# Token sums of a fast down projection made beside gate-up, the gated result added in DRAM, and wider modulation sums

## The chip, the cores and the metric

The program runs on one core of one Trainium2 chip. The metric is the device time of one execution in microseconds, as a median of several executions. TensorE is called PE here, VectorE DVE, ScalarE ACT, GpSimd POOL, and SyncE SP; SP does nothing but issue transfers.

## The reference

One layer of a diffusion backbone works on 640 tokens (512 latent tokens and 128 context tokens) of width 2048, all in float32. What matters here is the conditioning vector and the second half of the layer:

```
mod   = silu(c) @ w_ada + b_ada               # 6 parts of 2048, once for latent, once for context
x     = x + gate1 * mixed                     # mixed: attention and convolution through w_out
h2    = rms_norm(x, g_norm2) * (1 + scale2) + shift2
gte, up = split(h2 @ w_gate_up)               # 2 x 5632 columns
x     = x + gate2 * ((silu(gte) * up) @ w_down)
y     = rms_norm(x, g_final)
```

## The kernel before, in words

Features lie on the partitions and tokens on the free axis: a tile of 128 features holds two halves of 320 tokens (256 latent and 64 context tokens each). Every float32 operand of a product is split into a rounded high part (a float32r copy, made by ACT, line 143) and the remainder (a subtraction by DVE, line 144), and three matmuls (high-high, high-low, low-high) make the product.

Gate-up and down are computed with a 2x2 block scheme with seven products in place of eight (`seven`, line 715). It needs sums of the weights, made in `weights` (lines 702 to 712) by DVE, and sums of two token tiles: from the tiles b1 and b2 the four halves t3, n1, t2 and t4 (in `splits`, line 650). A *unit* is one weight tile of 512 KB and 42 matmuls that use 14 token tiles, the high and low parts of seven tiles for each of two pairs. The pool R has 57 slots of a token tile's size, and four units fill 56 of them.

The stages follow one another: an early part, the convolution projections, attention, the out projection in two halves of 16 rounds, gate-up (44 rounds of four units), down (26 *visits* of one to four units, 80 units in all), and a tail of 16 rounds in two passes, which multiplies the last four of the 44 middle tiles with a piece of w_down that is left over, adds it, and makes the final norm.

Around the change the work goes as follows:

- **Modulation** (`ada2`, line 256): the columns of w_ada for gate1, shift2, scale2 and gate2 are summed on DVE, 512 columns at a time. In each of 16 row blocks a multiply-add for each of two conditioning vectors goes over a tile of 128x512. `background(n)`, called by each weight split, hands out steps of this work at a rate that belongs to the stage (`RATES`). Twelve of the sixteen column blocks are handed out in the convolution and the first half of the out projection, four in gate-up.
- **Gate-up** stores each gated tile in DRAM (`mid`, line 749, on ACT's queue).
- **Down** joins a new unit every second visit. Four tiles of `mid` are loaded on SP's queue (line 767), POOL makes the four sums of each pair (lines 655 to 658), ACT and DVE split them (lines 143 and 144). A visit's seven products become two tiles by one ACT copy and seven DVE operations (lines 777 to 784), and both are stored or added in DRAM to `y` by a transfer on POOL's queue (lines 787 and 789).
- **Between down and tail** `y` and the residual `x1` come back from DRAM, DVE multiplies by gate2 and adds (line 802), four `mid` tiles are loaded and split, and 16 weight tiles for the tail are loaded and split (lines 804 to 815).

The order on each engine and queue is not the source order. A planner simulates the program and issues what is ready and lies first in the source; `after(x)` forces an instruction to stand behind x on its engine. Tiles of a tag share a number of buffers, and a tile waits until the buffer's earlier user is done.

Of the kernel before, what the change touches and what calls it, by code (L numbers as in the profile page):

```python
# [16 lines left out]
P = 128  # L17
# [12 lines left out]
WINDOW = KT // 2  # L30
S = 512
# [45 lines left out]
def _emit(nc, tc, pool, dram, a):  # L77
# [13 lines left out]

    def brief(n, name):

        return bpool.tile([P, n], F32, name=name, tag="D", bufs=bufs["D"])
# [25 lines left out]
    def two(ap, n):  # L120
        return ap.rearrange("p (j n) -> p j n", j=2)
# [54 lines left out]
    cc = pool.tile([P, KT, 2], F32, name="cc")  # L176
# [78 lines left out]

    def ada2(b):
        acc = [brief(512, "acc") for _ in range(2)]
        for q in range(8):
            ws = [T1(F32, (P, 512), "aw") if bufs is SECOND else brief(512, "aw") for _ in range(2)]
            for kk in range(2):  # L260
                nc.sync.dma_start(ws[kk], a["ada2"][b, q, :, kk])
            for kk in range(2):
                k = 2 * q + kk
                with after(newest[V]):
                    for v in range(2):
                        if k == 0:
                            V.tensor_scalar(acc[v], ws[kk], sc[:, k, v:v + 1], None, op0=ALU.mult)
                        else:
                            V.scalar_tensor_tensor(acc[v], ws[kk], sc[:, k, v:v + 1], acc[v],  # L269
                                                   op0=ALU.mult, op1=ALU.add)  # L270
                yield
        yield
        yield
        with after(newest[T]):
            pb = psB()
            for v in range(2):
                for j in range(4):
                    T.matmul(pb[32 * j:32 * j + 32, v * P:(v + 1) * P], ones[:, 0:32], acc[v][:, j * P:(j + 1) * P],
                             start=True, stop=True)
            ev = T2(F32, (P, 256), "ev")  # L280
            A.copy(ev, pb[:, 0:256])
        yield
        with after(newest[T]):
            for v in range(2):
                T.transpose(pb[:, 256 + v * P:256 + (v + 1) * P], ev[:, v * P:(v + 1) * P], ident)
            col = pb[:, 256:512].rearrange("p (v j x) -> p j v x", v=2, j=4)[:, :, :, 0]
            fs = slice(4 * b, 4 * b + 4)
            V.tensor_tensor(mod2[:, fs, :], col, bada[:, 4 * b:4 * b + 4, :], op=ALU.add)
            if 8 <= b < 12:
                g = cst("g2", KT, 2)[:, 4 * (b - 8):4 * (b - 8) + 4, :]  # L290
                V.scalar_tensor_tensor(mod2[:, fs, :], mod2[:, fs, :], 1.0, g, op0=ALU.add, op1=ALU.mult)

    def ada2_steps(blocks, overlap=True):
        prev = iter(())
        for b in blocks:
            gen = ada2(b)
            if not overlap:
                yield from gen
                continue
            for _ in range(16):  # L300
                next(gen)
                next(prev, None)
                yield b
            prev = gen
        for _ in prev:
            yield b

    steps = ada2_steps((0, 1, 2, 3, 4, 8, 5, 9, 6, 10, 7, 11))
# [341 lines left out]
    def splits(xs, n, wide):  # L650


        (b1, b2), e = xs, G if wide else V
        ta, tb = T1(F32, (P, 2, n)), T2(F32, (P, 2, n))
        e.tensor_tensor(ta[:, 0], b1[:, 1], b2[:, 1], op=ALU.subtract)
        e.tensor_tensor(ta[:, 1], b1[:, 1], b1[:, 0], op=ALU.subtract)
        e.tensor_tensor(tb[:, 0], b2[:, 1], ta[:, 1], op=ALU.subtract)  # L657
        e.tensor_tensor(tb[:, 1], b2[:, 0], tb[:, 0], op=ALU.subtract)  # L658
        out = {}
        one = R(F32R, (P, 2, n))  # L660
        split(one[:, 0], one[:, 1], b1[:, 0])
        out["b11"] = one[:, 0], one[:, 1]
        for t, names in ((b2, ("b21", "b22")), (ta, ("t3", "n1")), (tb, ("t2", "t4"))):
            hi, lo = R(F32R, (P, 2, n)), R(F32R, (P, 2, n))
            split(hi, lo, t)
            for k, name in enumerate(names):
                out[name] = hi[:, k], lo[:, k]
        return out

# [4 lines left out]
    for m in range(KT):  # L674
        add_gated(proj(a["w_out"][m], na, (1,)), ra, m)
        add_sq(ssq, x1[m], m == 0, G if m < KT - 2 else V)

        u = (T1 if m % 2 else T2)(F32, (P, 2, 322))
        for v, f in PARTS:
            A.mul(f(u), f(x1[m]), mod2[:, 32 + m, v:v + 1])  # L680
        G.tensor_copy(u[:, 0, 320:322], mod2[:, 16 + m, :])
        G.memset(u[:, 1, 320:322], 0.0)
        nc.scalar.dma_start(two(x1d[m], 320), x1[m])
        us.append(u)
        if m % 2:
            hs.append(splits(us, 322, False))
            us = []
# [8 lines left out]
    steps = ada2_steps((12, 13, 14, 15), False)  # L696
# [33 lines left out]
    mid = [dr(f"mid{i}", (P, 640)) for i in range(NMID)]  # L730
    credit[1] = RATES[4]
    for i in range(NMID):
# [16 lines left out]
        nc.scalar.dma_start(two(mid[i], 320), row(up))  # L749
    del hs, r2  # L750
    rest_of_background()
# [4 lines left out]
    y = [[dr(f"y{mp}_{i}", (P, 640)) for i in range(2)] for mp in range(KT // 2)]  # L756
    there = {}
    visits = 2 * (ND_U - 1) + WINDOW
    for n in range(visits):
        mp = n % (KT // 2)  # L760
        first = n < KT // 2
# [8 lines left out]
        units = [u for u in there if 2 * u <= n < 2 * u + WINDOW]  # L770
        ps = seven([(a["w_down"][u, n - 2 * u], there[u]) for u in units])
        for u in units:
            if n == 2 * u + WINDOW - 1:
                del there[u]
        ps = {k: p[:, 0:320] for k, p in ps.items()}
        u2, u3, ya, yb = brief(320, "u2"), brief(320, "u3"), T1(), T2()
        A.copy(u2, ps["p1"])
        V.tensor_tensor(ya[:, 0], ps["p2"], u2, op=ALU.add)
        V.tensor_tensor(u2, u2, ps["p6"], op=ALU.subtract)
        V.tensor_tensor(u3, u2, ps["p7"], op=ALU.subtract)  # L780
        V.tensor_tensor(yb[:, 0], ps["p4"], u3, op=ALU.subtract)
        V.tensor_tensor(u2, u2, ps["p5"], op=ALU.subtract)
        V.tensor_tensor(yb[:, 1], ps["p5"], u3, op=ALU.subtract)
        V.tensor_tensor(ya[:, 1], ps["p3"], u2, op=ALU.add)
        for i, yt in enumerate((ya, yb)):
            if first:
                nc.gpsimd.dma_start(two(y[mp][i], 320), yt)
            else:
                nc.gpsimd.dma_start(two(y[mp][i], 320), yt, accum_op=ALU.add)


    brief_pools.close()
    bpool, bufs = brief_pools.enter_context(tc.tile_pool(name="third", bufs=1, reuse_waits="tile")), THIRD
    x1 = [None] * KT
    for n in range(visits - KT // 2, visits):
        for i in range(2):
            m = 2 * (n % (KT // 2)) + i
            x1[m], t = R(), (T1 if i else T2)()
            nc.sync.dma_start(x1[m], two(x1d[m], 320))
            nc.sync.dma_start(t, two(y[m // 2][i], 320))  # L800
            for v, f in PARTS:
                V.scalar_tensor_tensor(f(x1[m]), f(t), mod2[:, 48 + m, v:v + 1], f(x1[m]), op0=ALU.mult, op1=ALU.add)
    mids = []
    for i in range(CHUNK):
        t = (T1 if i % 2 else T2)()
        nc.sync.dma_start(t, two(mid[NMID - CHUNK + i], 320))
        mids.append((R(F32R), R(F32R)))
        split(*mids[i], t)
# [7 lines left out]

    def rstd_tokens(ssq, n):

        ps, c = psB(), n // P
        v, t, y = (small([P, 3], s)[:, 0:c] for s in ("rv", "rt", "ry"))  # L820
# [13 lines left out]
    def out_y(ms, cs, n, off, rf):  # L834
        o = brief(len(ms) * n, "o").rearrange("p (m n) -> p m n", m=len(ms))
# [6 lines left out]
    for c0, c1, off in ((128, 320, 0), (0, 128, 384)):  # L842
        n = 2 * (c1 - c0)
        fssq = brief(n, "fssq")
# [70 lines left out]
def _arrays(i):  # L915
# [24 lines left out]
    d["ada2"] = np.ascontiguousarray(wa[:, 2 * D:].reshape(8, 2, P, 16, 512).transpose(3, 0, 2, 1, 4))  # L940
# [20 lines left out]
    order = (2 * np.arange(ND_U)[:, None] + np.arange(WINDOW)) % (KT // 2)  # L961
# [25 lines left out]
```

## Time and profile before

| | us |
|---|---|
| median of 3 runs | 2826.29 (2821.36 to 2830.71) |
| the profiled execution | 2827.13 |
| its span in the trace | 2825.3 |
| PE busy | 2697.7 (95% of the span) |
| DVE busy | 2255.1 (80%) |
| ACT busy | 992.1 (35%) |
| POOL busy | 412.7 (15%) |

PE is the engine that sets the time. Its idle stretches and the stretches of a low granted clock are few and lie at the joints between stages, so the stretch table and the waits of PE are what to read first, and then the chain of waits through two joints.

### The profile page before, as it was taken

The numbers are of one execution on the slowest core, as the hardware profiler recorded it, in microseconds if no ns is written. First come the engines' busy times: TensorE is split into PE (matmuls) and PEld (weight loads), VectorE is DVE, ScalarE is ACT, GpSimd is POOL, SyncE is SP. The second block draws the span as 40 slices with busy tenths as digits, with TensorE's granted clock in tenths as the row PEclk, the third lists the DMA queues.
The fourth block names the chain that finished last, engine by engine and source line by source line (L and its number), as shares of the span: only waits on it lengthen the run. The fifth ranks groups of instructions, "written<-read, shape, count | busy, mean of one in ns | idle before, by whom it ended". The sixth has DMA issues, their size and how long they took to land.

```text
span 2825.3 us, 46451 instructions
## 1 busy us (share of the span) xinstructions
PE 2697.7 (95%) x18840; PEld 2636.4 (93%) x18840; DVE 2255.1 (80%) x3482; ACT 992.1 (35%) x1459; POOL 412.7 (15%) x329
## 2 busy tenths in 40 slices
PE   8999999999989989999999999999997999999968
PEld 6889999999889979999999999999996899999968
DVE  5578989766778678888888888888888987777776
ACT  2223222225632453333333333333333443333323
POOL 1110000000000121111111111111112322212013
PEclk9999999999999999999999999999998999999989
DMA  8855555550054323333333333333333444544673
GB/s 319 290 188 167 182 168 178 174 161 16 20 177 154 113 87 107 111 114 108 112 116 112 104 114 117 110 110 116 107 114 123 133 148 120 129 127 130 187 190 107
DMA packets 149382, 385.57 MB, mean 136 GB/s; under 512 B 16112, under 2 KB 31920, under 8 KB 149168
## 3 DMA queue, kind: packets, MB, share of 16 engines
q1 hardware_dynamic: 127056, 343.12, 38.2%
q0 software_dynamic: 6464, 17.04, 3.2%
q10 hardware_dynamic: 15648, 22.45, 2.2%
q8 instruction: 147, 2.41, 0.3%
q14 instruction: 67, 0.55, 0.1%
HBM read 337.82 MB, written 44.73 MB: 135 GB/s over the span
## 4 chain that ended last, share of the span: by engine, by line
PE 85%; DMA 5%; DVE 5%; ACT 2%; issue 1%; POOL 1%; SPq 0%; DVEq 0%; POOLq 0%; ACTq 0%
PE bank L726 50%; PE psA L166 27%; PE bank L849 2%; DMA t<-mid 2%; PE psA L550 2%; DMA y<-t 1%; PE psB L244 1%; DVE wl L144 1%; DVE r L144 1%; PE psB L579 1%; ACT wh L143 1%; PE psB L574 0%; ACT r L143 0%; POOL t L658 0%; POOL t L657 0%
## 5 line engine op out<-in xcount | busy, mean ns | idle before, releaser
L726 PE MATMUL bank<-r,wh 128*128 128x320 f32 (+1 forms) x7168 | 1485.1, 313 | 40.5 <-ACT r L143 22.3
L726 PEld LDWEIGHTS bank<-r,wh 128*128 128x128 f32 x7168 | 1178.2, 190 | 54.6 <-ACT r L143 26.6
L726 PE MATMUL bank<-r,wl 128*128 128x322 f32 (+1 forms) x3584 | 955.9, 311 | 0.5 <-DVE wl L144 0.5
L166 PE MATMUL psA<-r,wh 128*128 128x322 f32 (+1 forms) x3584 | 691.7, 314 | 14.5 <-ACT wh L143 6.3
L726 PEld LDWEIGHTS bank<-r,wl 128*128 128x128 f32 x3584 | 639.8, 190 | 1.2 <-DVE wl L144 1.2
L166 PEld LDWEIGHTS psA<-r,wh 128*128 128x128 f32 x3584 | 568.3, 190 | 29.6 <-issue 9.8
L143 ACT CAST wh<-wr 128x768 fp32r<-128x768 f32 (+1 forms) x370 | 332.8, 901 | 631.2 <-PE psA L166 337.0
L143 ACT CAST wh<-ws 128x1024 fp32r<-128x1024 f32 x256 | 268.7, 1050 | 576.4 <-DVE ws L710 576.4
L144 DVE TENSOR_TENSOR wl<-wr,wh 128x768 fp32r<-128x768 f32 (+1 forms) x370 | 414.8, 1121 | 52.3 <-ACT wh L143 51.9
L144 DVE TENSOR_TENSOR wl<-ws,wh 128x1024 fp32r<-128x1024 f32 x256 | 323.6, 1264 | 157.2 <-ACT wh L143 156.8
L166 PE MATMUL psA<-r,wl 128*128 128x322 f32 (+1 forms) x1792 | 414.8, 313 | 0.3 <-DVE wl L144 0.3
L269 DVE SCALAR_TENSOR_TENSOR acc<-aw,sc,acc 128x512 f32<-128x512 f32 x480 | 341.0, 758 | 17.3 <-DMA aw<-ada 17.1
L166 PEld LDWEIGHTS psA<-r,wl 128*128 128x128 f32 x1792 | 302.7, 189 | 3.5 <-issue 3.0
L745 POOL TENSOR_TENSOR t<-t,r 128x640 f32<-128x640 f32 x44 | 90.2, 2050 | 929.6 <-DVE t L742 484.1
L708 DVE TENSOR_TENSOR ws<-wr 128x512 f32<-128x512 f32 x256 | 208.9, 816 | 2.1
L228 POOL TENSOR_TENSOR r<-r,t 128x640 f32<-128x640 f32 x42 | 74.0, 1762 | 841.1 <-ACT t L227 834.6
L710 DVE TENSOR_TENSOR ws<-ws,wr 128x256 f32<-128x256 f32 x256 | 126.4, 494 | 6.2
L143 ACT CAST r<-t 128x640 fp32r<-128x640 f32 (+4 forms) x118 | 77.4, 662 | 134.8 <-DMA t<-mid 65.6
L144 DVE TENSOR_TENSOR r<-t,r 128x640 fp32r<-128x640 f32 (+4 forms) x118 | 97.8, 840 | 33.4 <-ACT r L143 31.3
L709 DVE TENSOR_TENSOR ws<-ws,wr 128x256 f32<-128x256 f32 x256 | 119.0, 465 | 3.3
L372 DVE TENSOR_TENSOR r<-psA,r 128x644 f32<-128x644 f32 x64 | 52.6, 826 | 57.8 <-PE psA L166 57.7
L744 POOL TENSOR_TENSOR t<-t,r 128x640 f32<-128x640 f32 x44 | 86.0, 1955 | 28.0 <-DVE t L743 26.6
(185 smaller groups left out, 1820.9 us busy)
## 6 DMA issues: line engine op xcount, KB each, us to landing
wr<-w_gu SPq DMA_DIRECT2D x176, 512.0 KB, 3.6
aw<-ada SPq DMA_DIRECT2D x256, 256.0 KB, 3.1
wr<-w_down SPq DMA_DIRECT2D x80, 512.0 KB, 3.6
wr<-w_rest SPq DMA_DIRECT2D x62, 512.0 KB, 3.9
y<-t POOLq DMA_DIRECT2D x52, 320.0 KB, 4.9
wr<-ada SPq DMA_DIRECT2D x32, 512.0 KB, 4.6
r<-ada SPq DMA_DIRECT2D x64, 256.0 KB, 5.1
wr<-w_out SPq DMA_DIRECT2D x32, 512.0 KB, 3.9
```

Of the source, the lines that this page charges most:

```text
L143: A.copy(hi, src)
L144: return V.tensor_tensor(lo, src, hi.bitcast(F32), op=ALU.subtract)
L166: newest[T] = T.matmul(out[:, j, 0:n], w[p], x[q][:, j, 0:n], start=first and i == 0, stop=last and i == 2).ins
L228: e.tensor_tensor(acc, acc, qv, op=ALU.add)
L269: V.scalar_tensor_tensor(acc[v], ws[kk], sc[:, k, v:v + 1], acc[v], op0=ALU.mult, op1=ALU.add)
L550: T.matmul(ps[:, i2, 0:320], st[:, ts], mv[:, i2, :], start=i == 0, stop=i == 4)
L708: V.tensor_tensor(q[:, :, 0:2], b[:, :, 1:4:2], b[:, :, 0:1].broadcast_to([P, 2, 2, P]), op=ALU.add)
L709: V.tensor_tensor(q[:, :, 2], q[:, :, 1], b[:, :, 1], op=ALU.add)
L710: V.tensor_tensor(q[:, :, 3], q[:, :, 2], b[:, :, 2], op=ALU.add)
L726: newest[T] = T.matmul(ps[name][:, 0:n], w[p][:, kp, i, :], xs[kp][x][q][:, 0:n], start=u + kp + t == 0, stop=u == len(units) - 1 and kp + ...
L744: G.tensor_tensor(row(g), row(g), r2, op=ALU.mult)
L745: G.tensor_tensor(row(up), row(up), r2, op=ALU.mult)
```

## The change

- `ada2` sums 1024 columns at a time, in eight blocks. All eight are handed out before gate-up: the rates are 0.85 in the convolution and the first half of the out projection and 0.6 in its second half; gate-up has none.
- In gate-up the token sums of each pair are made at once, by DVE, and split by ACT and DVE; seven tiles for each pair go to DRAM on ACT's queue (`parts`). The last four middle tiles are split too and kept as `plain`.
- Down loads 14 finished tiles for a unit on POOL's queue, straight into R. The units join at the visits of `JOINS`, and there are 25 visits.
- The results of a visit are multiplied by gate2 on ACT and added to the residual `x1d` in DRAM by a transfer on POOL's queue, in every visit. `y` and the stage that brought it back are gone.
- The tail loads `plain` on POOL's queue without a split, and `x1` on SP's.

```diff
+JOINS = (0, 1, 2, 3, 8, 9, 10, 11, 16, 17)
-FIRST = dict(T1=4, T2=3, D=6, wr=4, wh=3, wl=3)
-SECOND = dict(T1=3, T2=2, D=2, wr=3, ws=1, wh=3, wl=3)
-THIRD = dict(T1=4, T2=4, D=10, wr=3)
+FIRST = dict(T1=4, T2=3, acc=2, aw=2, wr=3, wh=3, wl=3)
+SECOND = dict(T1=4, T2=3, wr=3, ws=1, wh=3, wl=3)
-RATES = (1.3, 0.0, 1.3, 0.0, 0.2)
+RATES = (0.85, 0.0, 0.85, 0.6)
...
     def ada2(b):
+        acc = [tagged("acc", (P, 1024)) for _ in range(2)]
+        for k in range(KT):
+            w = tagged("aw", (P, 1024))
+            nc.sync.dma_start(w, a["ada2"][b, k])
+            with after(newest[V]):
+                for v in range(2):
+                    if k == 0:
+                        V.tensor_scalar(acc[v], w, sc[:, k, v:v + 1], None, op0=ALU.mult)
+                    else:
+                        V.scalar_tensor_tensor(acc[v], w, sc[:, k, v:v + 1], acc[v], op0=ALU.mult, op1=ALU.add)
+            yield
...
+    def ada2_steps():
+        for b in (0, 1, 2, 4, 3, 5, 6, 7):
+            yield from ada2(b)
...
+    def sums(b1, b2, n):
         ta, tb = T1(F32, (P, 2, n)), T2(F32, (P, 2, n))
+        V.tensor_tensor(ta[:, 0], b1[:, 1], b2[:, 1], op=ALU.subtract)
+        V.tensor_tensor(ta[:, 1], b1[:, 1], b1[:, 0], op=ALU.subtract)
+        V.tensor_tensor(tb[:, 0], b2[:, 1], ta[:, 1], op=ALU.subtract)
+        V.tensor_tensor(tb[:, 1], b2[:, 0], tb[:, 0], op=ALU.subtract)
+        return ta, tb
...
+    parts = [dr(f"parts{i}", (P, 7, 640)) for i in range(2 * ND_U)]
+    plain = [dr(f"plain{i}", (P, 2, 640)) for i in range(CHUNK)]
+    def keep(dst, hi, t):
+        A.copy(hi, t)
+        V.tensor_tensor(t.bitcast(F32R), t, hi.bitcast(F32), op=ALU.subtract)
+        nc.scalar.dma_start(two(dst[0], 320), hi.bitcast(F32))
+        nc.scalar.dma_start(two(dst[1], 320), t)
...
-        nc.scalar.dma_start(two(mid[i], 320), row(up))
-    del hs, r2
-    rest_of_background()
+        if i >= NMID - CHUNK:
+            d = plain[i - NMID + CHUNK]
+            keep((d[:, 0], d[:, 1]), T2(F32R), row(up))
+        elif i % 2 == 0:
+            b1 = up
+        else:
+            d = parts[i // 2]
+            one = T2(F32R)
+            split(one[:, 0], one[:, 1], b1[:, 0, 0:320])
+            nc.scalar.dma_start(two(d[:, 0], 320), one.bitcast(F32))
+            for k, t in enumerate((up, *sums(row(b1), row(up), 320))):
+                keep((d[:, 2 * k + 1], d[:, 2 * k + 2]), T1(F32R), row(t))
...
-        if n % 2 == 0 and n // 2 < ND_U:
-            xs = []
-            for k in range(2):
-                bs = T1(), T2()
-                for e in range(2):
-                    nc.sync.dma_start(bs[e], two(mid[4 * (n // 2) + 2 * k + e], 320))
-                xs.append(splits(bs, 320, True))
-            there[n // 2] = xs
+        for u in range(ND_U):
+            if JOINS[u] == n:
+                there[u] = []
+                for i in (2 * u, 2 * u + 1):
+                    ts = [R(F32R) for _ in range(7)]
+                    for k, t in enumerate(ts):
+                        nc.gpsimd.dma_start(t, two(parts[i][:, k], 320))
+                    there[u].append(named(ts[0], *zip(ts[1::2], ts[2::2])))
...
-        for i, yt in enumerate((ya, yb)):
-            if first:
-                nc.gpsimd.dma_start(two(y[mp][i], 320), yt)
-            else:
-                nc.gpsimd.dma_start(two(y[mp][i], 320), yt, accum_op=ALU.add)
+        for i, t in enumerate((ya, yb)):
+            m = 2 * mp + i
+            for v, f in PARTS:
+                A.mul(f(t), f(t), mod2[:, 48 + m, v:v + 1])
+            nc.gpsimd.dma_start(two(x1d[m], 320), t, accum_op=ALU.add)
...
+    mids = [(R(F32R), R(F32R)) for _ in range(CHUNK)]
     for i in range(CHUNK):
+        for k, t in enumerate(mids[i]):
+            nc.gpsimd.dma_start(t, two(plain[i][:, k], 320))
...
+    x1 = [R() for _ in range(KT)]
+    for i in range(KT):
+        m = (2 * visits + i) % KT
+        nc.sync.dma_start(x1[m], two(x1d[m], 320))
```

## Rows read from the trace of the kernel before

**Rows 1.** Busy time, granted clock (PEclk, 1.00 is full) and DMA by stretch.

```profile
core 0: us, PE busy (x) PEld busy (x) DVE busy (x) ACT busy (x) POOL busy (x), PEclk, DMA share, GB/s
175.00:660.00 485.00, 481.84 (x3320) 476.50 (x3320) 397.16 (x610) 121.96 (x174) 13.15 (x7) 1.00 0.52 162
...
830.00:940.00 110.00, 110.00 (x770) 108.84 (x769) 85.31 (x127) 26.38 (x30) 2.15 (x4) 1.00 0.46 144
940.00:1048.00 108.00, 103.63 (x707) 103.37 (x705) 82.60 (x120) 56.84 (x89) 27.81 (x41) 0.99 0.34 111
...
1085.00:2166.00 1081.00, 1079.70 (x7283) 1076.05 (x7282) 929.75 (x1367) 376.41 (x476) 171.62 (x86) 1.00 0.35 112
2166.00:2196.00 30.00, 10.12 (x49) 7.80 (x48) 25.14 (x37) 9.59 (x14) 11.75 (x10) 0.60 0.42 125
2196.00:2724.00 528.00, 508.34 (x3338) 498.92 (x3336) 420.48 (x637) 198.38 (x253) 120.12 (x123) 0.98 0.50 139
2724.00:2751.00 27.00, 0.44 (x2) 0.30 (x2) 19.45 (x39) 3.77 (x6) 1.72 (x2) 0.58 0.93 304
2751.00:2811.00 60.00, 59.98 (x396) 59.76 (x395) 38.78 (x86) 23.68 (x48) 23.59 (x26) 0.96 0.29 96
```

**Rows 2.** What PE waited for, whole span: total us, times, longest.

```profile
PE bank L849 <- ACT r L143: 26.6, 1, 26.6
PE bank L726 <- ACT r L143: 22.3, 12, 7.7
...
PE bank L278 <- DVE acc L269: 7.5, 1, 7.5
```

**Rows 3.** Chain of waits at the joint of gate-up and down: start, us, what.

```profile
2181.33 5.38 DMA mid<-t
...
2191.14 6.67 PE bank L726 x29
```

**Rows 4.** The same chain at the joint of down and tail.

```profile
2725.42 9.21 DMA t<-y
...
2742.87 6.51 DMA t<-mid
```

**Rows 5.** Instructions on the tile acc (modulation sums) by stretch.

```profile
175.00:660.00 485.00, 5.79 (x144) 3.38 (x144) 216.86 (x322) 1.00 0.52 162
830.00:940.00 110.00, 1.29 (x32) 0.75 (x32) 31.89 (x46) 1.00 0.46 144
...
1085.00:2166.00 1081.00, 1.93 (x48) 1.13 (x48) 87.65 (x120) 1.00 0.35 112
```

**Rows 6.** Groups of DVE instructions by form: busy us, mean ns, idle before.

```profile
L269 DVE SCALAR_TENSOR_TENSOR acc<-aw,sc,acc 128x512 f32<-128x512 f32 x480 | 341.0, 758 | 17.3 <-DMA aw<-ada 17.1
...
L144 DVE TENSOR_TENSOR wl<-wr,wh 128x1024 fp32r<-128x1024 f32 x114 | 142.2, 1247 | 23.3 <-ACT wh L143 23.3
L144 DVE TENSOR_TENSOR r<-t,r 128x640 fp32r<-128x640 f32 x64 | 62.9, 988 | 26.6 <-ACT r L143 26.3
L737 DVE TENSOR_TENSOR t<-bank,t 128x322 f32<-128x322 f32 x44 | 21.4, 486 | 0.0
```

**Rows 7.** DMA in 2195 to 2350: packets, MB, share of 16 engines.

```profile
q1 hardware_dynamic: 5328, 16.26, 34.0%
q0 software_dynamic: 1280, 5.24, 9.2%
```

**Rows 8.** DMA in 2350 to 2620, and an issue group with KB and us to landing.

```profile
q0 software_dynamic: 2880, 6.55, 15.5%
...
y<-t POOLq DMA_DIRECT2D x20, 320.0 KB, 5.2
```

**Rows 9.** SP's queue at the joint of gate-up and down, in order of time.

```profile
2152.34 9.94 SPq L705 DMA_DIRECT2D wr<-w_down  x3
...
2175.09 2.34 SPq L767 DMA_DIRECT2D t<-mid  x2
```

**Rows 10.** An ACT multiplication by a column, 940 to 1050, by form.

```profile
L680 ACT ACTIVATE t<-r,mod 128x512 f32<-128x512 f32 x16 | 11.5, 721 | 14.8 <-DVE r L625 13.1 <-POOL r L228 1.7
```

More of the change, by code (lines that the diff above doesn't have):

```diff
@@ L173, in _emit @@
     newest = {}
-    cc = pool.tile([P, KT, 2], F32, name="cc")
+    cc = R(F32, (P, KT, 2))
     newest[nc.sync] = nc.sync.dma_start(cc, a["cc"]).ins
@@ new lines, in ada2 @@
+        for k in range(KT):
[8 more added lines that the diff above has]
+            yield
+        with after(newest[T]):
+            pb, pt = psB(), psB()
+            for h in range(2):
+                for v in range(2):
+                    for j in range(4):
+                        T.matmul(pb[32 * j:32 * j + 32, (2 * h + v) * P:(2 * h + v + 1) * P], ones[:, 0:32],
+                                 acc[v][:, (4 * h + j) * P:(4 * h + j + 1) * P], start=True, stop=True)
+            ev = T2(F32, (P, 512), "ev")
+            A.copy(ev, pb)
@@ new lines, in ada2 @@
+        yield
+        with after(newest[T]):
+            for c in range(4):
+                T.transpose(pt[:, c * P:(c + 1) * P], ev[:, c * P:(c + 1) * P], ident)
+            col = pt.rearrange("p (h v j x) -> p h j v x", h=2, v=2, j=4)[:, :, :, :, 0]
+            fs = slice(8 * b, 8 * b + 8)
+            V.tensor_tensor(mod2[:, fs, :].rearrange("p (h j) v -> p h j v", h=2), col,
+                            bada[:, fs, :].rearrange("p (h j) v -> p h j v", h=2), op=ALU.add)
+            if 4 <= b < 6:
+                g = cst("g2", KT, 2)[:, 8 * (b - 4):8 * (b - 4) + 8, :]
+                V.scalar_tensor_tensor(mod2[:, fs, :], mod2[:, fs, :], 1.0, g, op0=ALU.add, op1=ALU.mult)
@@ L272, in ada2 @@
         yield
         yield
[L274 to L291, printed above, removed]
@@ L309, in _emit @@
+    steps = ada2_steps()
     credit = [0.0, 0.0]
@@ L647, in _emit, with named @@
     del nv
-    def splits(xs, n, wide):
-        (b1, b2), e = xs, G if wide else V
+    def sums(b1, b2, n):
         ta, tb = T1(F32, (P, 2, n)), T2(F32, (P, 2, n))
[L655 to L665, printed above, removed]
+        V.tensor_tensor(ta[:, 0], b1[:, 1], b2[:, 1], op=ALU.subtract)
[3 more added lines that the diff above has]
+        return ta, tb
+    def named(one, b, ta, tb):
+        out = {"b11": (one[:, 0], one[:, 1])}
+        for (hi, lo), names in ((b, ("b21", "b22")), (ta, ("t3", "n1")), (tb, ("t2", "t4"))):
             for k, name in enumerate(names):
@@ L668, in splits @@
         return out
+    def splits(b1, b2, n):
+        ta, tb = sums(b1, b2, n)
+        one = R(F32R, (P, 2, n))
+        split(one[:, 0], one[:, 1], b1[:, 0])
+        parts = []
+        for t in (b2, ta, tb):
+            parts.append((R(F32R, (P, 2, n)), R(F32R, (P, 2, n))))
+            split(*parts[-1], t)
+        return named(one, *parts)
     ssq = R()
@@ L685, in _emit @@
         if m % 2:
[L686 removed]
+            hs.append(splits(*us, 322))
             us = []
```

75 lines of the change are left out of this document (12 added, 63 removed).

## The prediction

> **What bounds the kernel now.** I read the busy time by stretch first [rows 1]. The reader is to see that PE is the limit almost everywhere: in gate-up (1085 to 2166) it is busy 1079.7 of 1081 us at the full clock, so an edit there can lose time but win none. The gaps lie at the joints: 10 of 30 us busy between gate-up and down, 508 of 528 in down, 0.4 of 27 between down and tail. The list of PE's waits says who ends these gaps [rows 2]: one wait of 26.6 us for ACT's splits before the tail, twelve of 22.3 us in all for ACT's splits of token tiles in down, one of 7.5 us for the last modulation sums. The chains of waits name what stands behind these splits: at the first joint a middle tile's way through DRAM, with the first long run of down's matmuls at 2191.1 [rows 3]; at the second joint the reload of y and of mid [rows 4]. At both joints the granted clock falls to the lower of its two levels, 1.2 GHz, after PE has idled (mean 0.60 and 0.58 in these stretches), and stays there for some us after work resumes.
>
> The yardstick is a unit of 42 matmuls: 42 x 1079.70/7283 = 6.2 us [rows 1]. Down's 80 units are 498 us, but it runs from 2166 to 2724, 558 us: 60 over. From 2724 to the end at 2825.3 are 101 us, of which the tail's matmuls hold 60.
>
> **The change part by part.**
>
> *Modulation sums.* A 512-wide multiply-add takes DVE 341.0/480 = 0.71 us [rows 6]. A 1024-wide one isn't in the trace: between 0.71 (the second half free) and 1.42 (two narrow ones). I take 1.25, the 1024-wide subtraction of the same engine (142.2/114) [rows 6]. A block has 19 steps, 16 of them with two such operations, 2.5 us a step. Steps by the rates: 62 weight pieces x 2 x 0.85 = 105 in the convolutions, which is five blocks and 10 rows (90 row steps); 27 in the first half of the out projection (22 row steps), 19 in the second (16). In the convolutions DVE comes from 397.2 to 397.2 - 216.9 + 225 = 405 of 485 us [rows 1, 5]: hidden. In the first half from 85.3 to 85.3 - 31.9 + 55 = 108 of 110: it just fits. In the second half, which had none, 82.6 + 40 = 123 against 108: DVE becomes the bound and I charge 15 us. Ends: at 0.71 it is 105 of 108, no cost; at 1.42 it is 128, and the first half overruns by 6, so 26. Below nothing isn't possible, since PE is busy 213.6 of these 218 us. The transfers have the same bytes; each is twice as large.
>
> *Gate-up.* It loses 87.7 us of modulation sums [rows 5] and gains, for each of 20 pairs, four sums of 0.49 us, three 640-wide subtractions of 0.99 (the mean that [rows 6] has of them, most of them beside a busy POOL) and a 320-wide one of some 0.5: 5.4 us, 108 in all. DVE goes from 930 to 950 of 1081. In the second round of a pair it has (930 - 88)/44 + 5.4 = 24.5 of 24.6 us: covered only by the three weight buffers, 18.6 us of PE's work. ACT (376 of 1081 busy) gains 20 x 3.5 copies, some 50 us at the 0.72 of a 512-wide operation [rows 10], and issues 148 stores for 44; a store that waits for DVE's subtraction holds the next weight cast behind it on ACT, and the same buffers cover that. I charge 2 us, ends 0 and 15. SP and POOL get nothing new here.
>
> *Loads of a unit.* 14 transfers of 320 KB on POOL's queue replace four on SP's, four sums on POOL and the splits. Their price isn't in the trace. From below: POOL's plain stores of this size, 16 in 9.2% of 155 us, 0.89 us each of all 16 DMA engines [rows 7]. From above: its adding stores, 20 in 15.5% of 270 us, 2.09 us [rows 8]. A load cheaper than a plain store has no row that speaks for it. I take 1.06 us: SP's queue, 16.26 MB in 34.0% of 155 us, is 309 GB/s [rows 7], and is nearest since it is reads from DRAM into SBUF. At that rate a unit's weights are 1.7 us per 6.2, 27% of the engines, and two adding stores a visit of 25 us 17%.
>
> Start: the last gate-up round frees the slots of one unit each 6.2 us from 18.6 us before its end. A unit loads in 14 x 1.06/0.73 = 20.3 us and lands 3 us later (5.2 to landing less the 2.09 [rows 8]); nearly all 14 tiles are needed from the thirteenth matmul, 1.8 us into the unit. Unit 0 is there at +4.7, wanted at +1.8: 2.9 us. Unit 1 at 25.0, wanted at 17.1: 7.9. Unit 2 at 45.3 against 43.6: 1.7. Unit 3 in time. At visits 8 to 11 a load takes 14 x 1.06/0.56 = 26.5 us and has 39 from the slot's release to its use; each next one starts 1.6 us later: no stall. Together 12.5 us. The same walk gives 4 at 0.89, 30 at 1.2, 73 at 1.4, 118 at 1.6 and 229 at 2.09.
>
> The Trainium skill (DMA: Bandwidth & Descriptors, "SWDGE vs HWDGE vs iDMA") says that DMAs of all issuing engines run on the same 16 engines and interleave, so that another issuer saves only issue time; if instead POOL's queue were a road of its own, the walk would give no stall and the sum would be 13 us lower. The two queues' shares in [rows 7], of the same 16 engines, fit the rule and can't prove it. The same page's fit of 2.0 us plus bytes by 436 GB/s makes a load 0.75 us of transfer (an estimate); by it the sum is also 13 us lower, and no run here shows a load into a float32r tile.
>
> *Rest of down.* POOL's sums and the splits of the loaded tiles go (62.9 us of DVE for the 640-wide ones alone [rows 6]); ACT gains four multiplications a visit (0.72 for 512 wide [rows 10]), 2 us of 25. The waits for splits have nothing left to wait for. Late next are the loads. For short waits and a clock that is down at the start I leave 9 us (ends 0 and 25), so down takes 498 + 12.5 + 9 = 520 for 558: -38.
>
> *Joint with the tail.* The chain at 2719 to 2750 (last store of y, reload, mid, splits [rows 4]) goes: from visit 18 on only two units are in work, so 28 slots hold the split mids and ten of the tail's weights before down ends. What is late next is the last visit's residual: evicted in eight operations of 0.49 us [rows 6], multiplied in 1, added in 5.2 [rows 8] and reloaded in as much: some +16. PE fills eight PSUM banks in the meantime (8 x 12 of the tail's longer matmuls, about 15 us) and waits 2 or 3. The tail's 60 us were at a mean clock of 0.96 [rows 1]; at full clock 58. So 58 + 3 + 14 (the end, as before) = 75 for 101: -26. Ends: -30 without that wait; -10 if the reload behind twelve other x1 loads comes twice as late.
>
> **Sum**, against the profiled execution: 2825.3 + 15 + 2 - 38 - 26 = 2778 of span, 1.8 around it as before (2827.1 - 2825.3), 2780. The profiled execution lay 0.8 above the median of 2826.3, so the median comes to 2779 or 2780.
>
> **The rivals.**
>
> *Loads priced like adding stores.* Place: visits 0 to 3 and 8 to 11. It decides from 1.33 us a load, where the walk's stalls reach some 57 us and eat the gain; at 1.6 us the time is 2780 + 106 = 2886, at 2.09 it is 2996. For it: the only transfers of POOL's queue that do more than copy cost 2.09 [rows 8], and these write rounded float32r tiles. Against it: an adding store reads two places and writes one, a load reads one. Chance 0.17.
>
> *The loads stand behind the adding stores on POOL's queue,* as in the source: then each waits for the results of the visit before, some 9 us after its end, with all of the load exposed but the units in front: 206 us of stalls by the same walk, 2973. For it: POOL issues in order. Against it: SP issued three of down's weight loads 23 us before the first mid load, which stands ahead of them in the source [rows 9], so the queue goes by what is ready. Chance 0.06.
>
> *DVE costs more.* In the out projection DVE is full for both halves; if it also idles for ACT and PE a tenth of these 218 us, and some 8 us of its backlog stand in the joint with gate-up, the charge is 45 us for 15: 2810. For it: 25 of its 108 us in the second half were idle before [rows 1]. Against it: most of that was spare time. Chance 0.15.
>
> *Nothing stalls:* loads at 0.89, sums behind the other work: 2780 - 8 - 15 - 9 = 2748. For it: the rows of the plain stores. Against it: 123 us of DVE in 108. Chance 0.12.
>
> **How the numbers follow.** My forecast, 2765 to 2800, has 0.50. The range 2748 to 2870 leaves out most of the load rivals above (0.16) and little below (0.04). A measurement here can tell about 0.3%, 8.5 us, from no change. Faster: 0.50 + 0.12 and 0.11 of the DVE case, 0.73. Same: 0.04 of it and 0.03 of loads near 1.33 us, 0.07. Slower: the rest of the load cases, 0.20.
>
> **What would show it.** Right: PE's waits for ACT's splits gone at L726 and L849, a few us of waits for loads at the first joint, POOL's queue at about 1.06 us of the engines a load, DVE full between 940 and 1050, and PE's first tail matmul directly behind down's last. Wrong: PE waiting for loads at visits 9 to 11, POOL's queue near 2 us a load, or the loads in POOL's queue behind the stores of the same visit.

## The result, and the profile after

The changed kernel takes 2749.89 us (median of 4 runs, 2748.72 to 2752.00) where the kernel before takes 2826.99 beside it (4 runs): a ratio of 0.973, 95% interval 0.9712 to 0.9747, or 77 us less. The forecast was 2780, a gain of 46; the time lies inside the range of 2748 to 2870, at its lower end, and below the 2765 to 2800 of the likeliest case. The profiled execution takes 2750.71, its span is 2748.9, 76.4 shorter than before.

First the busy time by stretch, cut where the stages of the changed kernel begin and end; it answers to [rows 1].

```profile
175.00:660.00 485.00, 480.66 (x3338) 477.07 (x3337) 400.04 (x463) 122.97 (x172) 12.57 (x7) 1.00 0.55 173
...
830.00:940.00 110.00, 110.00 (x793) 108.50 (x793) 97.88 (x117) 26.81 (x30) 2.03 (x4) 1.00 0.59 186
940.00:1066.00 126.00, 110.34 (x749) 109.01 (x747) 118.27 (x149) 57.32 (x92) 38.66 (x41) 0.95 0.46 149
...
1103.00:2180.00 1077.00, 1077.00 (x7244) 1077.00 (x7243) 946.35 (x1419) 424.84 (x560) 169.72 (x108) 1.00 0.42 135
2180.00:2210.00 30.00, 26.51 (x170) 26.21 (x169) 21.51 (x37) 12.45 (x20) 17.01 (x28) 0.94 1.14 371
2210.00:2674.00 464.00, 464.00 (x3163) 464.00 (x3162) 334.82 (x533) 185.43 (x268) 93.67 (x146) 1.00 0.71 196
2674.00:2735.00 61.00, 61.00 (x420) 61.00 (x420) 34.95 (x82) 21.53 (x45) 26.27 (x30) 1.00 0.50 165
```

The reader is to see two things. In the second half of the out projection (940 to 1066) DVE is busy 118 of 126 us and PE only 110: this stretch was 108 us before, so the changed kernel loses 18 us here. After that PE hardly stops: all of 1077 us in gate-up, 26.5 of 30 at the joint, then 464 of 464 and 61 of 61, at the full clock. Down lasts 497.5 us (2180 to 2677.5) for 558, and from there to the end are 71.4 us for 101. By stage: +18 up to gate-up, -4 in gate-up, -60 in down, -30 behind it, together -76.

What PE waited for, over the whole span (total us, times, longest), answers to [rows 2].

```profile
PE psA L162 <- ACT r L139: 11.0, 3, 5.3
...
PE bank L715 <- DVE t L787: 3.5, 1, 3.5
...
PE bank L821 <- DVE r L860: 1.5, 1, 1.5
```

The waits of 26.6 us and of 22.3 us for ACT's splits, and the 7.5 us for the modulation sums, are gone. The largest new one stands in the out projection (11.0). No wait for a load of a unit is in the list. The chain of waits through the joint of down and tail answers to [rows 4]:

```profile
2659.88 17.78 PE bank L715 x121
2677.66 22.40 PE bank L847 x128
```

Two pieces, both PE, with no gap: the first tail matmul stands directly behind the last of down. SP's queue shows why: the tail's eight weight transfers and the first nine of the 16 residuals are requested before down's last matmul (2677.7).

```profile
2648.60 22.77 SPq L805 DMA_DIRECT2D wr<-w_tail  x8
2671.55 21.68 SPq L813 DMA_DIRECT2D r<-x  x16
```

The modulation sums by stretch, and one group by form (busy us, mean ns), answer to [rows 5, 6]:

```profile
175.00:660.00 485.00, 5.40 (x160) 4.06 (x160) 216.09 (x180) 1.00 0.55 173
...
830.00:940.00 110.00, 2.37 (x64) 1.56 (x64) 47.15 (x40) 1.00 0.59 186
940.00:1066.00 126.00, 1.08 (x32) 0.81 (x32) 37.72 (x27) 0.95 0.46 149
```

```profile
L262 DVE SCALAR_TENSOR_TENSOR acc<-aw,sc,acc 128x1024 f32<-128x1024 f32 x240 | 302.6, 1299 | 7.9 <-DMA aw<-ada 7.8
```

A 1024-wide multiply-add takes 302.6/240 = 1.26 us. POOL's queue over the whole span, then the queues and two groups of transfers (KB, median us to landing) from 2160 to 2230, answer to [rows 7, 8]:

```profile
q0 software_dynamic: 28512, 64.89, 9.2%
```

```profile
q0 software_dynamic: 8232, 18.76, 86.9%
q1 hardware_dynamic: 1448, 5.26, 20.2%
q10 hardware_dynamic: 832, 1.31, 5.4%
...
r<-parts POOLq DMA_DIRECT2D x54, 320.0 KB, 7.5
wr<-w_down SPq DMA_DIRECT2D x10, 512.0 KB, 7.0
```

The first line prices a load: 9.2% of 2748.9 us is 252.9; 50 adding stores, if they still cost 2.09 [rows 8], are 104.5 of it, and 148 loads (140 of units, 8 of the tail) share the rest, 1.00 us each. In the 70 us around the joint the shares add up to 1.12 of the same 16 engines, at a mean of 363 GB/s. When the loads are issued, POOL's timeline says (us, then what it waited for):

```profile
2154.88 1.31 POOL L774 DMA_DIRECT2D r<-parts  x2 [21.76 <-PE bank L715]
2158.96 4.97 POOL L774 DMA_DIRECT2D r<-parts  x9
...
2320.92 1.16 POOL L774 DMA_DIRECT2D r<-parts  x2 [20.67 <-PE bank L715]
2323.16 1.78 POOL L795 DMA_DIRECT2D x<-t  x2 [1.08 <-DVE wl L140]
```

The first go out 25 us before gate-up ends, each when PE frees its slot, and a later unit's loads stand ahead of the stores of the visit. So the rival in which they stand behind them fails.

### The profile page after: what moved, and what is told of

It is laid out like the page before. It is cut to its first block, busy times and chain, and to the rows that moved or that the text cites. A ratio compares the mean times of both kernels' runs of the same rounds, so it can differ in the third digit from the quotient of the medians.

```text
span 2748.9 us, 46698 instructions
## 1 busy us (share of the span) xinstructions
PE 2671.1 (97%) x18840; PEld 2625.9 (96%) x18840; DVE 2214.3 (81%) x3257; ACT 1024.5 (37%) x1550; POOL 402.5 (15%) x395
## 4 chain that ended last, share of the span: by engine, by line
PE 92%; DVE 4%; ACT 2%; issue 1%; DMA 1%; SPq 0%; ACTq 0%; DVEq 0%
PE bank L715 58%; PE psA L162 27%; PE bank L847 2%; PE psA L533 1%; PE psB L240 1%; DVE wl L140 1%; PE psB L562 1%; DVE acc L262 1%; DVE r L140 0%; PE psB L557 0%; ACT wh L139 0%; PE psB L269 0%; DMA t<-x 0%; DVE r L608 0%; ACT r L139 0%
## 5 line engine op out<-in xcount | busy, mean ns | idle before, releaser
L715 PE MATMUL bank<-r,wh 128*128 128x322 f32 (+1 forms) x7168 | 1594.5, 311 | 9.3 <-ACT wh L139 5.8
L715 PEld LDWEIGHTS bank<-r,wh 128*128 128x128 f32 x7168 | 1209.7, 189 | 10.6 <-ACT wh L139 6.8
L715 PE MATMUL bank<-r,wl 128*128 128x322 f32 (+1 forms) x3584 | 1112.8, 311 | 2.3 <-DVE wl L140 2.3
L715 PEld LDWEIGHTS bank<-r,wl 128*128 128x128 f32 x3584 | 678.5, 189 | 2.7 <-DVE wl L140 2.7
L140 DVE TENSOR_TENSOR wl<-ws,wh 128x1024 fp32r<-128x1024 f32 x256 | 366.0, 1430 | 31.2 <-ACT wh L139 31.1
L262 DVE SCALAR_TENSOR_TENSOR acc<-aw,sc,acc 128x1024 f32<-128x1024 f32 x240 | 302.6, 1299 | 7.9 <-DMA aw<-ada 7.8
L697 DVE TENSOR_TENSOR ws<-wr 128x512 f32<-128x512 f32 x256 | 177.4, 693 | 5.5
L698 DVE TENSOR_TENSOR ws<-ws,wr 128x256 f32<-128x256 f32 x256 | 108.0, 422 | 5.6
L699 DVE TENSOR_TENSOR ws<-ws,wr 128x256 f32<-128x256 f32 x256 | 108.8, 425 | 4.4
L774 POOL DMA_DIRECT2D r<-parts x140 | 77.2, 564 | 159.5 <-PE bank L715 105.4
L745 ACT ACTIVATE t<-t 128x512 f32<-128x512 f32 x88 | 44.8, 557 | 111.8 <-POOL t L742 111.8
```

Source lines behind the costliest of these rows:

```text
L140: return V.tensor_tensor(lo, src, hi.bitcast(F32), op=ALU.subtract)
L262: V.scalar_tensor_tensor(acc[v], w, sc[:, k, v:v + 1], acc[v], op0=ALU.mult, op1=ALU.add)
L697: V.tensor_tensor(q[:, :, 0:2], b[:, :, 1:4:2], b[:, :, 0:1].broadcast_to([P, 2, 2, P]), op=ALU.add)
L698: V.tensor_tensor(q[:, :, 2], q[:, :, 1], b[:, :, 1], op=ALU.add)
L699: V.tensor_tensor(q[:, :, 3], q[:, :, 2], b[:, :, 2], op=ALU.add)
L715: newest[T] = T.matmul(ps[name][:, 0:n], w[p][:, kp, i, :], xs[kp][x][q][:, 0:n], start=u + kp + t == 0, stop=u == len(units) - 1 and kp + ...
```

## The experiments

Each ratio to the kernel before has a 95% interval of some 0.0015 to either side, 4 us, so a difference of two runs is uncertain by some 6; medians are of 4 runs. Differences are to the changed kernel's 2749.9 where nothing else is said.

**e1_rates: the charge of the out projection alone.**

```
-RATES = (0.85, 0.0, 0.85, 0.6)
+RATES = (1.0, 0.0, 0.85, 0.05)
```

> The changed kernel with the modulation sums handed out at rates 1.0, 0, 0.85, 0.05: eight blocks are done by the end of the out projection's first half, nothing else differs. Theory A (the second half of the out projection became DVE's, and this costs 18 us, 126 for 108): that stage falls back to about 108 to 112 us while the convolutions (DVE 400 of 485) take 14 more rows of 2.6 us without a loss: 2733, within 4. Rival (the 18 us come from the transition and the order of the splits, not from DVE's load): 2746 to 2751. Second rival (the convolutions have no room, DVE there is as good as full): 2745 or more.

Measured: 2736.17, ratio 0.968 (0.9666 to 0.9695), 13.7 us less, as theory A has it. Busy time by stretch:

```profile
175.00:660.00 485.00, 480.99 (x3351) 474.68 (x3350) 434.11 (x493) 121.48 (x168) 14.17 (x7) 1.00 0.61 190
...
940.00:1052.00 112.00, 108.84 (x743) 108.57 (x741) 83.45 (x120) 56.58 (x88) 27.80 (x41) 1.00 0.34 109
```

The convolutions take 34 us more of DVE's work and PE is as busy there as before; the second half of the out projection takes 112 us, near the 108 before the change, and the wait of 11.0 us is gone. So the sums cost nothing where DVE has room, and 14 of the 18 us of loss came from the 0.6 in the second half; no run says where the other 4 come from. This version is the fastest of all, faster than both kernels: its interval and the changed kernel's do not meet.

**e2_512: the width of the sums.** Tiles of 128x512 with the rates doubled, so the same work falls into the same stages.

```
-        acc = [tagged("acc", (P, 1024)) for _ in range(2)]
+        acc = [tagged("acc", (P, 512)) for _ in range(2)]
...
-RATES = (0.85, 0.0, 0.85, 0.6)
+RATES = (1.7, 0.0, 1.7, 1.2)
```

> The changed kernel with the modulation sums in sixteen blocks of 512 columns, at doubled rates, so that the same columns fall in the same stages. Theory A (two narrow operations at 0.71 us against one wide of 1.26 us cost 0.16 us more a row and vector, 39 us over 480 narrow operations, of which those of the out projection, some 67 row pairs, are exposed): 7 to 14 us slower than the changed kernel, 2757 to 2764. Rival (the wide sums do nothing for the time, DVE has room everywhere): 2750. Rival (they are the main part of the gain): 2790 or more.

Measured: 2760.22, ratio 0.9765 (0.9749 to 0.9781), 10.3 us more, within theory A. The largest wait of PE is now for the sums:

```profile
PE psB L268 <- DVE acc L262: 8.6, 2, 6.3
```

The loss fits the shapes: [rows 6] give 0.71 us for 512 columns, so 1.42 for what the wide form does in 1.26. The narrow form also has twice as many transfers and closing steps, which this run doesn't part from the width.

**e8_mod: the modulation part in the kernel before**, at the rates of e1, with the changed kernel's buffer counts, and nothing else of the change.

```
-RATES = (1.3, 0.0, 1.3, 0.0, 0.2)
+RATES = (1.0, 0.0, 0.85, 0.05, 0.0)
```

> The kernel before, with the wide modulation sums all ahead of gate-up (rates 1.0, 0, 0.85, 0.05) and the buffers of the changed kernel in gate-up and down (T1 4 for 3, T2 3 for 2, the sums of an eviction in T1); gate-up, down and tail else as before. Theory A (down's gaps are the way of mid through DRAM, POOL's sums and the splits): it takes away the wait of 7.5 us for the last modulation sums at the joint and some of what follows it, 5 to 15 us, and down's waits for splits stay: 2811 to 2822. Rival (down's gaps were a lack of buffers, since POOL and the reloads waited for y's stores to free them): 2775 to 2795.

Measured: 2808.70, ratio 0.9941 (0.9927 to 0.9956), 17 us less than before: 2 below theory A, and not the rival's 2775 to 2795. PE's waits:

```profile
PE bank L836 <- ACT r L143: 26.6, 1, 26.6
PE bank L712 <- ACT wh L143: 15.0, 8, 5.8
PE bank L712 <- ACT r L143: 11.0, 10, 3.8
```

The 7.5 us for the modulation sums are gone, the splits in down cost half of their 22.3, and the 26.6 at the tail stand as they were. The waits for the weights' high parts (`wh`) grew; before they were

```profile
PE bank L726 <- ACT wh L143: 11.1, 7, 7.7
```

How the 17 us divide between the sums and the buffers, no run shows. From here to e1 are 72.5 us: the work that moved, the gated addition and the tail. The next runs divide them.

**e3_joins: units joining every second visit, as before.**

```
-JOINS = (0, 1, 2, 3, 8, 9, 10, 11, 16, 17)
+JOINS = (0, 2, 4, 6, 8, 10, 12, 14, 16, 18)
```

> The changed kernel with the units joining every second visit (0, 2, 4 ... 18; 26 visits), as before the change. Theory A (the joins cost nothing once the loads are finished tiles that arrive early; the joining visits only set how many visits there are): 2750, within 4; a visit more of one eviction is hidden. Rival (joining four units at once is what keeps PE fed, and every second visit leaves short visits in which DVE's evictions and weight splits of 8 us stand against 6.2 of PE): 2757 to 2775.

Measured: 2758.46, ratio 0.976 (0.9745 to 0.9774), 8.6 us more: the rival's time. PE's wait in down, and the stretch behind it:

```profile
PE bank L715 <- DVE t L784: 7.1, 1, 7.1
```

```profile
2195.00:2210.00 15.00, 11.54 (x60) 11.54 (x61) 7.96 (x18) 5.23 (x10) 7.50 (x14) 0.68 1.15 368
```

It does not wait for loads. Two visits of one unit each follow each other here; PE has done them before DVE has evicted the first, waits 7.1 us and then works for some us at a mean clock of 0.68. A later start of the loads bought nothing.

**a_mid: the middle tiles plain in DRAM, summed on POOL and split in down,** joins every second visit; gated addition, tail and modulations as changed.

```
-                    ts = [R(F32R) for _ in range(7)]
-                    for k, t in enumerate(ts):
-                        nc.gpsimd.dma_start(t, two(parts[i][:, k], 320))
+                    bs = T1(), T2()
+                    for k in range(2):
+                        nc.sync.dma_start(bs[k], two(mid[2 * i + k], 320))
+                    there[u].append(splits(*bs, 320))
```

> The changed kernel with its middle tiles as in the kernel before: stored plain in gate-up, loaded on SP's queue and summed on GpSimd and split in down, joins every second visit; gated addition, tail and modulations stay as changed. Theory A (the splits moved out of down are the largest part of the gain, about 43 us, on top of 8.6 for the joins): 2795 to 2805, the loss inside the visits of down. Rival (VectorE and GpSimd had room for the work in down, the gain is in the joins and the tail): about 2765.

Measured: 2780.41, ratio 0.9831 (0.9816 to 0.9846), 30.5 us more, 22 of it beyond e3. That is half of theory A's 43, and its place was wrong too. From 2170 to 2240 PE waits

```profile
PE bank L716 <- ACT r L139: 13.1, 6, 9.8
```

of the 16.1 us of such waits in the whole kernel, and by stretch

```profile
2180.00:2210.00 30.00, 18.02 (x103) 17.00 (x104) 24.71 (x33) 12.50 (x20) 12.68 (x11) 0.77 0.31 96
2210.00:2240.00 30.00, 24.88 (x140) 22.52 (x139) 25.01 (x37) 14.79 (x25) 12.34 (x13) 0.89 0.59 140
```

PE idles 17 of these 60 us and the clock falls to a mean of 0.77 and 0.89, worth 30 x 0.23 + 30 x 0.11 = 10 us at most. Of the next 260 us PE idles 4. So the gain of splitting ahead lies mostly at the first joint, hardly in the later visits.

**e4_y: y in DRAM, reloaded and gated before the tail;** the tail's tiles still come split.

```
-            for v, f in PARTS:
-                A.mul(f(t), f(t), mod2[:, 48 + m, v:v + 1])
-            nc.gpsimd.dma_start(two(x1d[m], 320), t, accum_op=ALU.add)
+            if n < KT // 2:
+                nc.gpsimd.dma_start(two(y[m], 320), t)
+            else:
+                nc.gpsimd.dma_start(two(y[m], 320), t, accum_op=ALU.add)
```

> The changed kernel, but down's results go to y in DRAM, stored in the first eight visits and added later, and are brought back, multiplied by gate2 and added on DVE ahead of the tail, as before the change; the tail's split tiles and weights are still loaded during the last visits. Theory A (the joint with the tail cost 30 us for two reasons, the reload of y behind its last store and the tail's own loads behind that; the second is the larger, since PE waited for a split of mid and not for x1): most of the 30 us stay won, 2752 to 2760. Rival (the gated addition in DRAM is what closes the joint): 2770 to 2780, PE waiting some 20 to 30 us at the tail's first matmuls.

Measured: 2770.99, ratio 0.9803 (0.9789 to 0.9818), 21 us more: the rival's time, though not at the tail's first matmuls. PE's wait, and three pieces of the chain behind the last store:

```profile
PE bank L827 <- DVE r L866: 20.2, 2, 18.7
```

```profile
2673.16 9.10 DMA y<-t
...
2682.32 5.97 DMA t<-y
...
2690.78 6.52 DMA t<-y
```

Every tail round can multiply, since its tiles and weights are there; what is late is the first pass's norm, which needs all 16 results and so the whole reload.

**a_ypool: e4_y with a third set of buffers ahead of the tail,** as in the kernel before.

```
+    brief_pools.close()
+    bpool, bufs = brief_pools.enter_context(tc.tile_pool(name="third", bufs=1, reuse_waits="tile")), SECOND
     mids = [(R(F32R), R(F32R)) for _ in range(CHUNK)]
```

> The changed kernel with y in DRAM as in e4_y, and besides a third set of buffers opened ahead of the tail as in the kernel before: the tail's weights, its y tiles and their splits wait for the last work of down. Between e8_mod and e1_rates lie 72.5 us; a_mid gives back 30.5 of them and e4_y 21, so 21 are without a cause. Theory A (the new set of buffers is that cause: the tail's weights can't be loaded and split ahead): about 21 over e4_y, 2787 to 2795, with a wait of PE for the splits of the tail's weights at the joint. Rival (y's way is the longest at the joint anyway, the weights come behind it; the 21 us lie elsewhere): within 5 of e4_y, 2767 to 2776.

Measured: 2783.46, ratio 0.9851 (0.9835 to 0.9868), 12.5 us over e4_y: between the two, nearer theory A. The weights' loads on SP's queue, and PE's waits at this joint:

```profile
2658.30 1.75 SPq L809 DMA_DIRECT2D wr<-w_tail  x3
2660.22 18.40 SPq L819 DMA_DIRECT2D t<-y  x7
2678.71 13.16 SPq L809 DMA_DIRECT2D wr<-w_tail  x5
```

```profile
PE bank L829 <- DVE r L868: 19.4, 2, 17.8
...
PE bank L855 <- DVE r L861: 7.5, 1, 7.5
```

Down's matmuls end at 2675.0 here; five of the eight weight transfers start 3.7 us or more after that, and PE waits another 7.5 us. The kernel before has these transfers in its chain too, between the two pieces of [rows 4]:

```profile
2734.65 8.16 DMA wr<-w_tail
```

Of the 72.5 us, then, a_mid gives back 30.5 (8.6 of it the joins), e4_y 21.1 and the set of buffers 12.5. Some 8 are left, little more than these differences are uncertain by; the splits of the tail's four tiles, which no run undid by themselves, may hold them. Parts undone one at a time need not add up.

**e7_tailfirst: the kernel before with the tail's tiles and weights ahead of y's reload** and ahead of the third set of buffers.

```
     mids = []
     for i in range(CHUNK):
         t = (T1 if i % 2 else T2)()
...
+    brief_pools.close()
+    bpool, bufs = brief_pools.enter_context(tc.tile_pool(name="third", bufs=1, reuse_waits="tile")), THIRD
+    x1 = [None] * KT
```

> The kernel before, with the tail's loads and splits of mid and of its weights put ahead of the reload of y and x1; all else as before. Theory A, as the run with y in DRAM left it (of the 30 us at this joint some 20 are y's reload and some 10 the tail's own loads behind it): 2815 to 2820. Rival (PE waited for the split of mid, so this alone closes the joint): 2797 to 2802.

Measured: 2835.94, ratio 1.0038 (1.0023 to 1.0053), 10 us slower than before, where both theories had it faster.

```profile
PE bank L823 <- DVE fssq L862: 20.5, 1, 20.5
PE bank L849 <- ACT r L143: 13.7, 1, 13.7
```

The wait of 26.6 became 13.7, and 20.5 us for the norm came in its place. Splits and y's reload are two paths to the same joint: taking one from the head of the other moves the wait. Of the runs here, only those that shorten both close it.

**e5_behind: the loads forced behind the last adding store of the visit before,** as the rival of the prediction had them.

```
+                        with after(*stored):
+                            nc.gpsimd.dma_start(t, two(parts[i][:, k], 320))
...
+            stored[:] = [nc.gpsimd.dma_start(two(x1d[m], 320), t, accum_op=ALU.add).ins]
```

> The changed kernel, with each unit's loads forced behind the last adding store of the visit before on POOL's queue (the first unit's excepted). Theory A (the loads are free because the queue issues them a visit early, as slots come free): units 1 to 9 then wait 11 to 21 us each, 110 to 130 us in all by the walk of the prediction with a load at 0.95 to 1.06 us and the engines' shares as the trace after has them; 2860 to 2880. Rival (the order is of no weight, the transfers are quick enough anyway): 2750 to 2765.

Measured: 2781.29, ratio 0.9849 (0.9834 to 0.9863), 31 us more.

```profile
PE bank L715 <- DMA r<-parts: 15.9, 17, 5.3
```

```profile
2180.00:2260.00 80.00, 68.42 (x401) 64.51 (x401) 46.15 (x73) 25.36 (x36) 29.15 (x49) 0.89 0.81 250
```

PE does wait for the loads now, 15.9 us in 17 waits, and up to 2260 the mean clock is 0.89. The direction is the walk's, its size is far off. A unit's 14, which then come at one time, take some 18 us (the engines are full from 2366 to 2384, at up to 405 GB/s). But unit 4's go out 3 us behind the last eviction of the visit before (2361.5 to 2364.7), and not the 9 of the prediction (one of that visit's two stores stands before them, the other among them). Their last tile lands at 2388.3, and PE comes to the unit at some 2380, but it idles only some 0.3 us there: from 2380.4 to 2393.0 it starts 82 matmuls, of which the unit has 42, so other work fills the time.

**e6_double: a copy from DRAM to DRAM of the same size behind each load,** on POOL's queue.

```
-                        nc.gpsimd.dma_start(t, two(parts[i][:, k], 320))
+                        load_of = nc.gpsimd.dma_start(t, two(parts[i][:, k], 320)).ins
+                        with after(load_of):
+                            nc.gpsimd.dma_start(dr(f"again{i}_{k}", (P, 640)), parts[i][:, k])
```

> The changed kernel, with a copy of the same bytes from DRAM to DRAM issued behind each load on POOL's queue, so that a load costs the DMA engines about twice as much (the copies' results are not used). The prediction's walk (slots free 18.6 us ahead, engines shared to a sum of 1.0) says 210 us at 2 us a load: 2960. The walk as the trace after has it (first loads 25 us ahead, as single tiles come free in the round's first unit, and shares that add to 1.13) says 100 us: 2850. Rival (the DMA has so much room that the price of a load is of no weight): 2750 to 2765.

Measured: 2806.05, ratio 0.9932 (0.9914 to 0.9949), 56 us more.

```profile
PE bank L715 <- DMA r<-parts: 22.6, 20, 3.8
```

```profile
2180.00:2260.00 80.00, 62.50 (x304) 55.36 (x303) 35.36 (x58) 20.57 (x32) 46.83 (x81) 0.79 1.08 371
```

POOL's queue takes 13.0% of 2801 us, 364 for 253, so a copy is 0.79 us and a load with its copy 1.8 times a load. At that price the stalls come: 17.5 us of idle and a mean clock of 0.79 in 80 us. But the walk asked for two to four times as much.

**a_noload: units 4 to 9 load nothing** and multiply the tiles of the unit four before.

```
+                    if u >= 4:
+                        there[u].append(kept[u - 4, i % 2])
+                        continue
```

> The changed kernel, where units 4 to 9 of down reuse the split tiles of the unit four before and load nothing (the values of these units are not the reference's). Theory A (the loads are hidden but for 1 or 2 us): 2748 to 2751. Rival (the loads take time from other transfers, and so from TensorE): faster by more than 5, under 2745.

Measured: 2752.00 (2750.05 to 2754.48), ratio 0.9731 (0.9717 to 0.9746): no gain from 84 loads fewer. The loads of these units are hidden whole. POOL's queue:

```profile
q0 software_dynamic: 16416, 37.36, 6.3%
```

That is 173 us of the engines for 253, 0.95 us for each load left out, a second price beside the 1.00.

**a_sumsG: the token sums of gate-up on POOL.**

```
-        V.tensor_tensor(ta[:, 0], b1[:, 1], b2[:, 1], op=ALU.subtract)
+        e = G if n == 320 else V
+        e.tensor_tensor(ta[:, 0], b1[:, 1], b2[:, 1], op=ALU.subtract)
```

> The changed kernel with the token sums of gate-up on GpSimd in place of VectorE. Theory A (VectorE is not what ends gate-up, so it makes no difference who sums): 2750, within 4. Rival (the sums on VectorE cost gate-up time, or GpSimd's own slowness delays the splits): more than 5 either way.

Measured: 2749.75 (2748.12 to 2752.49), ratio 0.9724 (0.9707 to 0.9741): the same, and DVE was not even relieved. One DVE group in gate-up of the changed kernel, and the same of this one with one of POOL's:

```profile
L140 DVE TENSOR_TENSOR wl<-ws,wh 128x1024 fp32r<-128x1024 f32 x173 | 264.4, 1528 | 27.3 <-ACT wh L139 27.2
```

```profile
L140 DVE TENSOR_TENSOR wl<-ws,wh 128x1024 fp32r<-128x1024 f32 x174 | 288.5, 1658 | 11.8 <-ACT wh L139 9.9
...
L639 POOL TENSOR_TENSOR t<-t,t 128x320 f32<-128x320 f32 x20 | 34.7, 1735 | 0.0
```

DVE's busy time in gate-up rises from 946 to 961 us although 80 subtractions of 0.48 (39 us) left it. PE is busy 1077 of 1077 us either way.

## Why the prediction was right, and where its sizes were off

**What held.** The sign, the places, and the mechanism: PE's waits for ACT's splits go at both joints, the loads hide, DVE fills the second half of the out projection, and the tail's first matmul stands behind down's last. Term by term, forecast against measured: modulations +15, +18; gate-up +2, -4; down -38, -60; joint and tail -26, -30. That the time lies in the range owes something to luck: it is 2 us above the lower end, and it missed the likeliest case by 15.

**Modulations.** 1.25 us for the unseen wide multiply-add, measured 1.26; 123 us of DVE in the second half, measured 118 busy in a stretch of 126. The charge fits what e1 gives back (13.7). PE's own wait in that stretch is for ACT's splits (11.0); that it goes away with the sums, in e1, ties it to them. The stretch is longer than DVE's work: its idle us there are the small part of the "costs more" rival that is true.

**The term that was mis-sized is down,** by 22 of the 30 us that the whole missed. I had left 60 - 38 = 22 us over the 498 of its units; the measurement, 497.5, leaves none. Some 5 of that is the yardstick, which I took from gate-up: down's units take 42 x 464.00/3163 = 6.16 us, 493 in all. The price of a load was right (1.06 for 1.00). What failed is the walk, in the step "a unit loads in 14 x 1.06/0.73 = 20.3 us" from "18.6 us before its end":

- The 0.73 took the weights' share off, as if shares of the engines could not pass 1. They do: 0.87 for POOL's queue beside 0.20 and 0.05 for the others, which makes 14 x 1.00/0.87 = 16.1 us a unit. In the trace the loads of units 1, 2 and 3 begin 13, 18 and 18 us after those of the unit before.
- The first slots come free 25 us before gate-up's end, tile by tile, not a unit at a time. With both, the last tiles of units 0, 1 and 2 land at -2, 13 and 31 us from gate-up's end in the trace. By the walk without a stall they are wanted at 2, 14 and 33 (the 17 and 44 of the prediction had its stalls in them): no stall, as measured, but unit 1 is in time by some 1 us. By the walk (an estimate), the earlier start alone, or a pace of 18 us alone, would leave some 6 of the 12.5 us.
- A unit does not need nearly all its tiles at once: by the order of its products ten of the 14 are needed from the thirteenth matmul, and the last four later. Where loads really were late (e5, e6) PE waited in 17 and 20 short waits, and the loss was 31 and 56 us, where the prediction's walk has 206 and 210. My upper rivals, 2886 and 2973, were too dear for the same reason; the second of them, made true in e5, costs 2781.
- Of the 9 us for short waits and a low clock some 5 came: PE idles 3.5 us at the first joint, and the mean clock is 0.94 in its 30 us (30 x 0.06 = 2) and 1.00 after.

The Trainium skill (DMA: Bandwidth & Descriptors, "SWDGE vs HWDGE vs iDMA") has all issuers share 16 engines and interleave; the trace agrees, since in the 70 us in which POOL's queue holds 0.87 of them a weight of SP's queue takes 7.0 us to landing for 4.5 over the whole span. It is the arithmetic of shares that was mine. The 0.75 us a load that the prediction works out from the same page's fit isn't borne out by the 1.00 and 0.95 measured here.

**The tail** came in at the end of my bounds that I had given for "without that wait". The last residual's way through DRAM is there, 19 us for the 16 of the prediction: it lands at 2696.5, down's last matmul ends at 2677.7. But DVE adds the tail's first result at 2684.0, so rounds whose residual was back earlier go first; PE waits 1.5 and 1.2 us in the whole tail.

**The time agrees with the rival "nothing stalls" (2748), its reasons don't.** That one had the modulations free and the loads at 0.89. The modulations cost all 18 us; down and tail gave it back.

**Gate-up** gained 4 where I charged 2: with all modulation sums ahead of it, PE is busy all of 1077 us. It no longer idles there (1.3 us before [rows 1]) and no longer multiplies for the sums (1.9 us [rows 5]); its DVE at 946 of 1077 ends nothing (a_sumsG).

## What to carry to other kernels

Work that stands between a store and the first matmuls of a stage is worth moving to the stage that makes the data, even at 3.5 times the transfers (14 for 4 a unit), as long as the slots for the results come free before the stage begins; the gain is at the joint, and the low clock behind it goes with it. Where two paths end at one joint, shorten both: putting one ahead of the other won nothing (e7). And look for what holds the loads back: with y in DRAM, the opening of a new set of buffers was worth 12 us. Work handed out at a rate belongs to the stage whose engine has room; one that is full by sum is already too late.

## What the runs showed that I had not expected

- The shares of the queues add up to 1.12 over 70 us (1.18 in 15 us of e3_joins, at 402 GB/s): a queue's own rate says little of what all of them get together. SP's queue moved 309 GB/s over the share that it held [rows 7].
- A load from DRAM into float32r tiles on POOL's queue costs 1.00 us of all engines for 320 KB (0.95 in a_noload), less than half of an adding store of that size (2.09).
- Work on POOL slows DVE beside it. In gate-up the 1024-wide subtraction (`wl<-ws`) takes DVE 1.22 us where no POOL operation overlaps it and 2.1 to 2.5 where one does: 131 and 42 times in the changed kernel, 91 and 83 in a_sumsG, hence the means of 1.53 and 1.66. POOL itself takes 1.43 to 1.74 us for a subtraction that DVE does in 0.48.
